# Two decoder layers on one core: the p product's groups issued between the seven products of the first gate/up blocks

## The chip, the cores and the metric

The kernel runs on one core of a Trainium2 chip. The metric is the device time of one execution in microseconds, the median of several runs; lower is better.

## What is computed

Two layers of a decoder trunk over 512 positions with width 1024, in float32. Each layer has a mixer (spatial gating, retention, forgetting attention), a gated MLP with a causal convolution of width 3 on the gate branch, and a last step that multiplies a projection of a per-layer input `p` with a gate:

```python
mix = jnp.concatenate([out_a.astype(dt), out_b, out_c], axis=-1) @ w_o[i]
x = x + rmsnorm(mix, mix_post_g[i])

h = rmsnorm(x, ffn_pre_g[i])
f = conv_gated_mlp(h, w_gate[i], w_up[i], conv_w[i], conv_b[i], w_down[i])
x = x + rmsnorm(f, ffn_post_g[i])

gate = jax.nn.sigmoid(rmsnorm(x, ple_pre_g[i]) @ w_ple_gate[i])
e = p[i] @ w_ple_proj[i]
x = x + rmsnorm(e * gate, ple_post_g[i])
```

The product that the change moves is `e = p[i] @ w_ple_proj[i]`: 512 x 256 times 256 x 1024. It depends on inputs alone and is needed only in the layer's last step.

## The kernel before

**Precision.** Each float32 operand is split into a high half (a cast on ScalarE, ACT) and a low half (a subtraction on VectorE, DVE) by `split` (line 648). Each product of two 128-deep operands is then three matmuls: high by high, high by low, low by high (`mm3`, line 908).

**The p product.** `embed_operands` (line 1352) loads and splits p and the weights. `embed` (line 1386) makes the product in groups, one for each half of 512 columns and each chunk of 128 positions: 6 matmuls of 512 columns into a PSUM bank named eps, a copy on ACT to a tile e, and a store of e to DRAM on SyncE's queue (SP). Layer 0 makes one column half there (4 groups, 24 matmuls; the other half has been made at the start of the program), layer 1 both (8 groups, 48 matmuls). `ffn` (line 1250) calls `embed` ahead of its loop over blocks.

**The MLP.** `ffn` has 32 gate/up blocks. Each makes 128 columns of gate and 128 of up for all 512 positions by seven block products in place of eight (`seven`, line 860), of 12 matmuls of 256 columns each, into three banks: beta, alpha, gamma. The order of the seven, by the operand of the activations, is b11 (beta), b21 (alpha), h6 (beta), hd (gamma), h7 (beta), b22 (gamma), h4 (beta). In the profile b11, b21 and b22 read hb, h6, h7 and h4 read hh, and hd reads hhd. Between products ACT and DVE copy the banks' partial sums out to gs and us, since a product that adds to the same bank has to wait for the copy. The weights of a block come as raw tiles (graw, two loads of 512 KB on SP), two adds by GpSimd's DMA (POOL), and splits into wg, wu, wsa and wsb. From block 4 on, matmuls of the down projection (bank dn, weights traw and thl) stand between the products; blocks 0 to 3 have none.

**The operands of the seven products** come from the normed activations in chunks of 128 positions, in the order 0, 2, 1, 3 (`Seven`, line 754). Each chunk is scaled on DVE (h), transposed on TensorE (PE, two groups of four into a bank hps), and split. Chunks 0 and 1 give b11 and b21; chunks 2 and 3, with 0 and 1, give h6, hd, h7, b22 and h4. So b11 and b21 are whole after chunk 1, and the other five after chunk 3.

**The order of the work.** Instructions are not issued as the code is written: they are recorded, and `Plan.issue` (line 252) orders each engine's by a model of durations. Among instructions that are ready and for which a buffer is free, the one recorded first goes first. PE is bound to the recorded order only from block 4 on (`plan.fence(True)`, line 1329). A tile is given out only to instructions within a distance of the oldest unfinished one, by the stage (`AHEAD`, line 62: 503 for emb, 443 for gu0). The order is fixed when the program is built; each engine then runs its own list, and waits where an operand is not there. Every recorded operation bears line 452 in the profile, so it is read by the names of tiles.

Of the kernel before, what the change touches and what calls it, by code (L numbers as in the profile page):

```python
# [39 lines left out]
NCH = 4  # L40
# [491 lines left out]
def body(ctx, tc, a, out):  # L532
    nc = tc.nc
    plan = Plan(tc)
# [18 lines left out]
    def bank(name="ps"):  # L553
        return ppt([P, 512], F32, tag="ps", name=name, bufs=8)
# [4 lines left out]
    def b8(name, shape, dt=F32):  # L559
        kind = "W" if name in ("wg", "wsa", "wsb") else "X" if dt == F32R else None  # L560
        return b8t([P] + list(shape), dt, name, kind)
# [295 lines left out]
        split(sb[:, 0, :], sb[:, 1, :], raw[:, 1024:2048])  # L857
        return wg, wu, sa, sb

    def seven(h, ws, gs, us, scale=1.0, between=None):  # L860

        wg, wu, sa, sb = ws
        be, al, ga = (bank(n)[:, 0:256] for n in ("beta", "alpha", "gamma"))
        t1, t2 = slice(0, 256), slice(256, 512)

        def product(ps, w, n, first, last, part=range(4)):
            for k in part:
                ks = slice(k * P, k * P + P)
                mm3(ps, lambda i: w[i][:, ks], lambda i: h.part(n, i, k), first and k == 0, last and k == 3, True)

        def part(t, i):
            return [t[:, j, i * 512:i * 512 + 512] for j in range(2)]
        product(be, part(wg, 0), "b11", True, False)
        A.copy(gs[:, t1], be)
        product(al, part(wg, 1), "b21", True, True)
        V.tensor_tensor(out=gs[:, t1], in0=al, in1=gs[:, t1], op=ALU.add)
        product(be, part(sa, 0), "h6", False, False)
        A.copy(gs[:, t2], be)
        product(ga, part(sa, 1), "hd", True, False)
        if scale == 1.0:  # L880
            A.copy(us[:, t2], ga)
        else:
            A.mul(us[:, t2], ga, -scale)
        product(be, part(sb, 0), "h7", False, False)
        V.scalar_tensor_tensor(out=us[:, t2], in0=be, scalar=-scale, in1=us[:, t2], op0=ALU.mult, op1=ALU.subtract if scale == 1.0 else ALU.add)
        product(ga, part(sb, 1), "b22", False, True)
        V.tensor_tensor(out=gs[:, t2], in0=ga, in1=gs[:, t2], op=ALU.add)
        rest = between() if between else None
        product(be, wu, "h4", False, True, range(1) if rest else range(4))
        if rest:  # L890
            rest()
            product(be, wu, "h4", False, True, range(1, 4))
        A.mul(us[:, t1], be, -scale)
# [14 lines left out]
    def mm3(ps, lhs, rhs, first, last, skip=False):  # L908
        for i, (h, r) in enumerate(((0, 0), (0, 1), (1, 0))):
            T.matmul(ps, lhsT=lhs(h), rhs=rhs(r), start=first and i == 0, stop=last and i == 2, skip_group_check=skip)  # L910
# [339 lines left out]
    def ffn(l, hs, emb, ready, x, new, g, nxt):  # L1250
# [7 lines left out]
        facc = []  # L1258
        acts = {}

        def gate_up(b, between):
            ws = gate_up_weights(l, b) if b not in ready else ready[b]
            gs, us = wk("gs"), wk("us")
            seven(hs, ws, gs, us, between=between)

            cv = wk("cv")
            A.activation(cv, gs, AF.Identity, bias=cw[:, 3, b:b + 1], scale=cw[:, 2, b:b + 1])
            V.scalar_tensor_tensor(out=cv[:, 1:S], in0=gs[:, 0:S - 1], scalar=cw[:, 1, b:b + 1], in1=cv[:, 1:S], op0=ALU.mult, op1=ALU.add)
            V.scalar_tensor_tensor(out=cv[:, 2:S], in0=gs[:, 0:S - 2], scalar=cw[:, 0, b:b + 1], in1=cv[:, 2:S], op0=ALU.mult, op1=ALU.add)
            A.activation(cv, cv, AF.Gelu_apprx_tanh)  # L1270
            V.tensor_tensor(out=cv, in0=cv, in1=us, op=ALU.mult)
            if b % 2 == 0:
                acts[b // 2] = b8("act", (2, 2, S), F32R)
            t = acts[b // 2]
            split(t[:, 0, b % 2, :], t[:, 1, b % 2, :], cv)
# [44 lines left out]
                rest = down(q - 1, c, units[q, hf], add)  # L1320
            return rest

        plan.stage = "emb"
        embed(l, *emb)
        plan.stage = "gu0"
        for b in range(31):
            if b == 4:
                plan.stage = "gu"
                plan.fence(True)
            gate_up(b, lambda: pieces(b))  # L1330
        plan.fence(False)
        gate_up(31, lambda: None)
        pieces(31)()
# [2 lines left out]
        us = [wd(7, hf) for hf in range(2)]  # L1336
# [46 lines left out]
                plan.fence(not c2)  # L1383
        return pT, us

    def embed(l, pT, us, chunks=range(NCH)):

        for hf, u in us.items():
            cs = slice(hf * 512, hf * 512 + 512)
            e = b8("e", (NCH, 512))  # L1390
            for c in chunks:
                ps = bank("eps")
                ts = slice(c * P, c * P + P)
                for k in range(2):
                    mm3(ps, lambda i: pT[:, i, k, ts], lambda i: u[:, i, k, :], k == 0, k == 1)
                A.copy(e[:, c, :], ps)
                SY.dma_start(out=ed[l][:, c, cs], in_=e[:, c, :])

    ov = out[0].rearrange("(c p) d -> p c d", p=P)

# [91 lines left out]
    for l in range(DEPTH):  # L1492
# [3 lines left out]
        hs = Seven(g)  # L1496
        emb = out_proj(l, cc, ready, Rows(src), xd[3 * l], g, hs)
# [36 lines left out]
```

## Time and profile before

| | us |
|---|---|
| timed runs, median of 3 | 1567.31 |
| lowest and highest timed run | 1564.96, 1567.66 |
| profiled execution, span from the first to the last instruction | 1564.8 |
| PE busy, DVE busy, ACT busy, POOL busy | 1546.8, 1219.5, 888.6, 193.3 |
| p product of layer 1 on PE, first to last start | 1012.8 to 1024.5 |

The page gives no time for the profiled execution other than its span. In rows of the profile, "beta<-hb,wg" means that bank beta is written from operand hb and weights wg; a bracket at the end says how long the engine had been idle before the row and what ended that. PEld is the loading of weights into TensorE, SPq and POOLq are queues of DMA issues. A start is given in us from the start of the span.

### The profile page before, as it was taken

The numbers are of one execution on the slowest core, as the hardware profiler recorded it, in microseconds if no ns is written. First come the engines' busy times: TensorE is split into PE (matmuls) and PEld (weight loads), VectorE is DVE, ScalarE is ACT, GpSimd is POOL, SyncE is SP. The second block draws the span as 40 slices with busy tenths as digits, with TensorE's granted clock in tenths as the row PEclk, the third lists the DMA queues.
The fourth block names the chain that finished last, engine by engine and source line by source line (L and its number), as shares of the span: only waits on it lengthen the run. The fifth ranks groups of instructions, "written<-read, shape, count | busy, mean of one in ns | idle before, by whom it ended". The sixth has DMA issues, their size and how long they took to land.

```text
span 1564.8 us, 26898 instructions
## 1 busy us (share of the span) xinstructions
PE 1546.8 (99%) x10554; PEld 1401.3 (90%) x10554; DVE 1219.5 (78%) x2036; ACT 888.6 (57%) x1501; POOL 193.3 (12%) x233
## 2 busy tenths in 40 slices
PE   9999999999999999999999999999999999999997
PEld 6998878999899999998889898799999999999986
DVE  6778978977778778767796789799677788687685
ACT  8556647765554545535584576586555455455362
POOL 1111112101101111000120101121101011011010
PEclk9999999999999999999999999999999999999999
DMA  9444529545637446456474346295546455455641
GB/s 331 92 123 104 180 90 291 134 121 142 169 81 198 137 96 176 130 156 247 155 216 102 85 122 210 76 301 136 145 112 155 143 136 147 128 150 148 232 158 54
DMA packets 87877, 239.00 MB, mean 153 GB/s; under 512 B 10036, under 2 KB 18364, under 8 KB 87752
## 3 DMA queue, kind: packets, MB, share of 16 engines
q1 hardware_dynamic: 64856, 195.81, 36.0%
q0 software_dynamic: 22464, 40.90, 16.4%
q8 instruction: 82, 1.34, 0.3%
q10 hardware_dynamic: 432, 0.59, 0.1%
q14 instruction: 43, 0.35, 0.1%
HBM read 219.94 MB, written 17.33 MB: 152 GB/s over the span
## 4 chain that ended last, share of the span: by engine, by line
PE 91%; ACT 3%; DMA 3%; DVE 2%; issue 1%; SPq 0%; POOLq 0%; POOL 0%; DVEq 0%; ACTq 0%
PE beta L452 26%; PE dn L452 21%; PE ps L452 14%; PE gamma L452 13%; PE alpha L452 6%; PE wo L452 3%; DMA graw<-in_w_gu_dram 2%; PE hps L452 1%; PE sps L452 1%; PE tps L452 1%; PE ops L452 1%; PE eps L452 1%; PE gps L452 1%; ACT thl L452 1%; PE rops L452 1%
## 5 line engine op out<-in xcount | busy, mean ns | idle before, releaser
L452 PE MATMUL dn<-thl,act 128*128 128x512 f32 x1536 | 370.5, 391 | 0.0
L452 PEld LDWEIGHTS dn<-thl,act 128*128 128x128 f32 x1536 | 280.4, 188 | 52.3
L452 PE MATMUL ps<-thl,hT 128*128 128x512 f32 (+3 forms) x984 | 209.7, 368 | 1.1 <-ACT hT L452 0.9
L452 POOL DMA_DIRECT2D graw<-in_w_gu_dram x128 | 112.4, 917 | 759.0 <-DVE wg L452 162.2
L452 PEld LDWEIGHTS ps<-thl,hT 128*128 128x128 f32 x984 | 175.1, 188 | 25.0 <-ACT hT L452 1.5
L452 DVE TENSOR_TENSOR thl<-traw,thl 128x1024 fp32r<-128x1024 f32 (+3 forms) x124 | 142.3, 1155 | 19.3 <-ACT thl L452 19.2
L452 ACT CAST thl<-traw 128x1024 fp32r<-128x1024 f32 (+3 forms) x124 | 121.3, 995 | 22.0 <-DVE wsb L452 8.9
L452 PEld LDWEIGHTS beta<-hh,wu 128*128 128x128 f32 x936 | 125.6, 188 | 9.1
L452 PE MATMUL beta<-hh,wu 128*128 128x256 f32 x936 | 130.2, 279 | 0.0
L452 PE MATMUL beta<-hh,wsa 128*128 128x256 f32 x936 | 122.0, 279 | 1.2 <-ACT gs L452 0.8
L452 PE MATMUL beta<-hh,wsb 128*128 128x256 f32 x936 | 120.5, 278 | 2.0 <-ACT gs L452 1.5
L452 PE MATMUL gamma<-hhd,wsa 128*128 128x256 f32 x936 | 121.7, 278 | 0.0
L452 DVE TENSOR_TENSOR wsb<-graw,wsb 128x1024 fp32r<-128x1024 f32 x78 | 95.3, 1222 | 29.5 <-PE beta L452 16.8
L452 PEld LDWEIGHTS beta<-hh,wsa 128*128 128x128 f32 x936 | 113.4, 188 | 2.6 <-ACT gs L452 1.4
L452 PEld LDWEIGHTS beta<-hh,wsb 128*128 128x128 f32 x936 | 112.9, 188 | 2.8 <-ACT gs L452 2.1
L452 DVE TENSOR_TENSOR graw<-graw 128x512 f32<-128x512 f32 x156 | 106.3, 686 | 10.8 <-DMA graw<-in_w_gu_dram 8.3
L452 PEld LDWEIGHTS gamma<-hhd,wsa 128*128 128x128 f32 x936 | 113.8, 188 | 0.0
L452 DVE TENSOR_TENSOR facc<-dn,facc 128x512 f32<-128x512 f32 x112 | 77.0, 687 | 45.1 <-PE dn L452 44.8
L452 DVE TENSOR_TENSOR wg<-graw,wg 128x1024 fp32r<-128x1024 f32 x78 | 95.2, 1220 | 15.8 <-ACT wg L452 8.7
L452 DVE TENSOR_TENSOR wsa<-graw,wsa 128x1024 fp32r<-128x1024 f32 x78 | 95.2, 1220 | 14.7 <-ACT wsa L452 14.6
L452 PE MATMUL beta<-hb,wg 128*128 128x256 f32 x768 | 100.5, 278 | 1.3 <-DVE hb L452 0.8
L452 DVE SCALAR_TENSOR_TENSOR cv<-gs,cw,cv 128x511 f32<-128x511 f32 (+1 forms) x128 | 95.3, 745 | 7.5 <-ACT cv L452 7.1
(225 smaller groups left out, 2625.4 us busy)
## 6 DMA issues: line engine op xcount, KB each, us to landing
graw<-in_w_gu_dram SPq DMA_DIRECT2D x128, 512.0 KB
graw<-in_w_gu_dram POOLq DMA_DIRECT2D x128, 256.0 KB, 5.4
traw<-in_w_dn_dram SPq DMA_DIRECT2D x64, 512.0 KB
x<-x SPq DMA_DIRECT2D x40, 512.0 KB
graw<-in_w_fm_dram SPq DMA_DIRECT2D x28, 512.0 KB
traw<-in_w_wo_dram SPq DMA_DIRECT2D x16, 512.0 KB
traw<-in_w_pg_dram SPq DMA_DIRECT2D x16, 512.0 KB
graw<-in_w_fm_dram POOLq DMA_DIRECT2D x28, 256.0 KB, 4.7
```

The lines of the kernel that those rows point to most:

```text
L452: made = o[1](*[self.map(v) for v in o[2]], **{k: self.map(v) for k, v in o[3].items()})
```

## The change

`embed` becomes a generator, `embed_pieces`, that stops after each group. `ffn` makes the generator and gives it to the first four blocks; `seven` draws one group from it behind its second product and one behind its fourth. So eight groups at most are recorded in blocks 0 to 3; layer 0 has four, which go to blocks 0 and 1. They are recorded under the stage gu0, no longer emb.

```diff
-    def seven(h, ws, gs, us, scale=1.0, between=None):
+    def seven(h, ws, gs, us, scale=1.0, between=None, wide=None):
...
         product(al, part(wg, 1), "b21", True, True)
         V.tensor_tensor(out=gs[:, t1], in0=al, in1=gs[:, t1], op=ALU.add)
+        if wide is not None:
+            next(wide, None)
         product(be, part(sa, 0), "h6", False, False)
         A.copy(gs[:, t2], be)
         product(ga, part(sa, 1), "hd", True, False)
...
             A.mul(us[:, t2], ga, -scale)
+        if wide is not None:
+            next(wide, None)
         product(be, part(sb, 0), "h7", False, False)
...
-        def gate_up(b, between):
+        def gate_up(b, between, wide=None):
             ws = gate_up_weights(l, b) if b not in ready else ready[b]
             gs, us = wk("gs"), wk("us")
-            seven(hs, ws, gs, us, between=between)
+            seven(hs, ws, gs, us, between=between, wide=wide)
...
-        plan.stage = "emb"
-        embed(l, *emb)
+        wide = embed_pieces(l, *emb)
         plan.stage = "gu0"
         for b in range(31):
             if b == 4:
                 plan.stage = "gu"
                 plan.fence(True)
-            gate_up(b, lambda: pieces(b))
+            gate_up(b, lambda: pieces(b), wide if b < 4 else None)
...
-    def embed(l, pT, us, chunks=range(NCH)):
+    def embed_pieces(l, pT, us, chunks=range(NCH)):
 
         for hf, u in us.items():
             cs = slice(hf * 512, hf * 512 + 512)
-            e = b8("e", (NCH, 512))
+            e = None
             for c in chunks:
+                e = b8("e", (NCH, 512)) if e is None else e
                 ps = bank("eps")
...
                 SY.dma_start(out=ed[l][:, c, cs], in_=e[:, c, :])
+                yield
+
+    def embed(*args):
+        for _ in embed_pieces(*args):
+            pass
```

What the planner makes of it: every engine's order is the same in both programs up to the gate/up blocks of layer 1. PE in layer 1, from chunk 1's second transposes, before (the number behind a name tells tiles apart; beta_11078 is block 0's bank, hps_11092 and hps_11105 are chunk 3's transposes):

```order
L452 MATMUL hps_11021<-k_ident_80,h_11006 128x128 x4
L452 MATMUL eps_11004<-ehl_10611,pT_10595 128x512 x2
L452 MATMUL eps_11032<-ehl_10611,pT_10595 128x512 x6
L452 MATMUL eps_11047<-ehl_10611,pT_10595 128x512 x6
L452 MATMUL eps_11058<-ehl_10611,pT_10595 128x512 x6
L452 MATMUL beta_11078<-hb11_10823,wg_10663 128x256 x8
L452 MATMUL hps_11092<-k_ident_80,h_11076 128x128 x4
L452 MATMUL beta_11078<-hb11_10823,wg_10663 128x256 x3
L452 MATMUL hps_11105<-k_ident_80,h_11088 128x128 x4
```

And in the changed program, from the same row (beta_11043 and alpha_11068 are block 0's, beta_11046 and alpha_11108 block 1's; hps_11119 and then hps_11130 are chunk 3's):

```order
L452 MATMUL hps_11021<-k_ident_80,h_11006 128x128 x4
L452 MATMUL eps_11004<-ehl_10611,pT_10595 128x512 x2
L452 MATMUL eps_11035<-ehl_10611,pT_10595 128x512 x3
L452 MATMUL beta_11043<-hb11_10823,wg_10663 128x256
L452 MATMUL beta_11046<-hb11_10823,wg_11018 128x256
L452 MATMUL eps_11035<-ehl_10611,pT_10595 128x512 x2
L452 MATMUL beta_11043<-hb11_10823,wg_10663 128x256 x11
L452 MATMUL alpha_11068<-hb21_10838,wg_10663 128x256
L452 MATMUL beta_11046<-hb11_10823,wg_11018 128x256 x3
L452 MATMUL alpha_11068<-hb21_10838,wg_10663 128x256 x11
L452 MATMUL beta_11046<-hb11_10823,wg_11018 128x256 x8
L452 MATMUL alpha_11108<-hb21_10838,wg_11018 128x256 x6
```

Thirteen matmuls of p have left this place, and 42 matmuls of blocks 0 and 1 stand ahead of chunk 3's first transposes, where 8 stood; behind chunk 3's second transposes (hps_11130) follow three alpha_11108, eleven of block 2's beta, and then the first with hhd. Of the matmuls that left, one stands behind block 0's h6 product, six ahead of block 3's h6 and six ahead of its h7. ACT in the same stretch, from the copy of the first eps of the second half, before:

```order
L452 COPY e_11060<-eps_11004 128x512
L452 COPY e_11060<-eps_11032 128x512
L452 COPY e_11060<-eps_11047 128x512
L452 CAST wg_11080<-graw_10947 128x1024
L452 COPY e_11060<-eps_11058 128x512
L452 CAST wu_11103<-graw_10947 128x512
L452 COPY s22_11115<-hps_11105 128x512
L452 COPY gs_11124<-beta_11078 128x256
L452 CAST hb22_10909<-s22_11115 128x4x128
L452 CAST hhd_10905<-sd_11118 128x4x128
L452 CAST hh7_10943<-s7_11129 128x4x128
L452 CAST hh6_10926<-s6_11139 128x4x128
```

And in the changed program (wg_11070 is block 2's gate weights, wg_11166 block 3's):

```order
L452 CAST wg_11070<-graw_10933 128x1024
L452 COPY gs_11084<-beta_11043 128x256
L452 CAST wu_11089<-graw_10933 128x512
L452 COPY e_11096<-eps_11004 128x512
L452 COPY gs_11111<-beta_11046 128x256
L452 COPY s22_11140<-hps_11130 128x512
L452 CAST hhd_10905<-sd_11128 128x4x128
L452 CAST hb22_10909<-s22_11140 128x4x128
L452 CAST wg_11166<-graw_11023 128x1024
L452 CAST hh6_10926<-s6_11154 128x4x128
L452 CAST hh7_10946<-s7_11180 128x4x128
```

Three copies of e have left, block 2's cast stands ahead, and block 3's cast has come ahead of h6's. On DVE, in the same way, block 2's wg now comes ahead of chunk 3's two h. SP in layer 1, from the stores of e's first column half, before:

```order
L452 DMA e_10964<-e 128x512 x4
L452 DMA x_10787<-x 128x1024
L452 DMA graw<-in_w_gu_dram 128x1024
L452 DMA e_10964<-e 128x512 x3
L452 DMA graw<-in_w_gu_dram 128x1024
L452 DMA e_10964<-e 128x512
L452 DMA graw<-in_w_gu_dram 128x1024 x2
L452 DMA traw<-in_w_dn_dram 128x1024 x2
L452 DMA graw<-in_w_gu_dram 128x1024 x4
L452 DMA traw<-in_w_dn_dram 128x1024 x2
```

And in the changed program:

```order
L452 DMA e_10964<-e 128x512 x4
L452 DMA graw<-in_w_gu_dram 128x1024 x2
L452 DMA x_10787<-x 128x1024
L452 DMA e_10964<-e 128x512
L452 DMA graw<-in_w_gu_dram 128x1024
L452 DMA e_10964<-e 128x512
L452 DMA graw<-in_w_gu_dram 128x1024
L452 DMA traw<-in_w_dn_dram 128x1024 x2
L452 DMA graw<-in_w_gu_dram 128x1024 x4
L452 DMA traw<-in_w_dn_dram 128x1024
L452 DMA e_10964<-e 128x512
L452 DMA traw<-in_w_dn_dram 128x1024
```

Block 3's two loads have come ahead of the store of x; the four stores of e's second half stand apart, one ahead of each of block 4's two loads, and one on each side of the last load of traw shown.

## The prediction

> **What bounds the kernel now.** I read the page's busy line first, then the busy time by stretches of the second layer, then PE's waits, then the rows of each engine around the p product.
>
> ```profile
> PE 1546.8 (99%) x10554; PEld 1401.3 (90%) x10554; DVE 1219.5 (78%) x2036; ACT 888.6 (57%) x1501; POOL 193.3 (12%) x233
> ```
>
> TensorE (PE) is busy for 1546.8 of 1564.8 us, so only the 18 us in which it is idle can be won without removing matmuls, and the change removes none. Where is that idle time? The stretches below show the window, then its length and PE's busy time, (instructions), the same for weight loads, DVE, ACT and POOL, and last the clock, DMA share and GB/s. The two run from the first product of p in layer 1 to block 7 of the gate/up blocks:
>
> ```profile
> 1012.80:1024.73 11.93, 11.93 (x58) 9.89 (x57) 10.49 (x18) 10.86 (x22) 4.59 (x6) 1.00 1.00 325
> 1024.73:1120.00 95.27, 95.26 (x746) 91.97 (x745) 82.32 (x117) 66.29 (x105) 14.36 (x17) 1.00 0.67 184
> ```
>
> PE has no idle time in the first and 0.01 us in the second. From 1075 us to the end PE waits for another engine once, 0.6 us for an ACT copy:
>
> ```profile
> PE beta L452 <- ACT gs L452: 0.6, 1, 0.6
> ```
>
> So in layer 1 PE is full where the p product stands, and full behind it.
>
> **What the change moves.** The order of the changed program is the same as before on every engine through layer 0: there the four groups of p (24 matmuls) stand in one piece ahead of the first block in both. In layer 1, 33 of 48 matmuls of p still come ahead of the first gate/up matmul; two come two matmuls later, one inside block 0, and twelve in block 3, six ahead of its third product and six ahead of its fifth. So the change, in effect, takes 15 matmuls, about a third of the second layer's p product, out of the piece that stands between chunk 1's and chunk 3's transposes, and moves products of blocks 0 and 1 forward into the hole. No instruction is added or removed on PE. The sum of its work is unchanged, and the question is only whether the products that move forward find their operands.
>
> *The gap behind chunk 1's transposes.* PE's rows of layer 1 (start, length, what):
>
> ```profile
> 1012.80 6.16 PE L452 MATMUL eps<-ehl,pT 128*128 128x512 f32 x26
> ...
> 1019.71 0.60 PE L452 MATMUL hps<-k_ident,h 128*128 128x128 f32 x4
> 1020.06 4.84 PE L452 MATMUL eps<-ehl,pT 128*128 128x512 f32 x20
> 1024.73 1.11 PE L452 MATMUL beta<-hb,wg 128*128 128x256 f32 x8
> 1025.85 0.66 PE L452 MATMUL hps<-k_ident,h 128*128 128x128 f32 x4
> ```
>
> Twenty p matmuls take 1024.73 - 1020.06 = 4.67 us, 0.2335 each, and today they cover the splitting of chunk 1. Thirteen of them go. What they cover, on ACT, DVE and POOL:
>
> ```profile
> 1020.00 0.58 ACT L452 CAST hb<-hps 128x512 fp32r<-128x512 f32 x1
> ...
> 1021.09 0.69 DVE L452 TENSOR_TENSOR hb<-hps,hb 128x512 fp32r<-128x512 f32 x1 [0.29 <-ACT bt L452]
> ...
> 1022.83 0.68 DVE L452 TENSOR_TENSOR hb<-hps,hb 128x512 fp32r<-128x512 f32 x1
> ...
> 1022.96 1.58 ACT L452 COPY e<-eps 128x512 f32<-128x512 f32 x3
> ...
> 1024.12 0.89 POOL L452 TENSOR_TENSOR rs<-vh,minus_half 128x1 f32<-128x1 f32 x1
> 1024.38 1.11 ACT L452 CAST wg<-graw 128x1024 fp32r<-128x1024 f32 x1
> ...
> 1025.04 1.42 DVE L452 SCALAR_TENSOR_TENSOR h<-x,rs,gain 128x512 f32<-128x512 f32 x2 [1.46 <-POOL rs L452]
> ```
>
> And layer 0, which already runs without the second half's matmuls, so that its products of blocks 0 and 1 follow chunk 1's transposes as they now will in layer 1:
>
> ```profile
> 251.88 0.38 PE L452 MATMUL beta<-hb,wg 128*128 128x256 f32 x1 [0.29 <-ACT hb L452]
> ...
> 252.35 0.69 DVE L452 TENSOR_TENSOR hb<-hps,hb 128x512 fp32r<-128x512 f32 x1 [0.54 <-ACT bt L452]
> ...
> 253.09 1.54 PE L452 MATMUL beta<-hb,wg 128*128 128x256 f32 x11 [0.83 <-DVE hb L452]
> ...
> 256.59 0.77 PEld L452 LDWEIGHTS beta<-hb,wg 128*128 128x128 f32 x6 [0.34 <-DVE wg L452]
> ...
> 258.19 0.60 PE L452 MATMUL hps<-k_ident,h 128*128 128x128 f32 x4
> ...
> 260.27 0.28 PE L452 MATMUL gamma<-hhd,wsa 128*128 128x256 f32 x1
> ...
> 262.25 0.68 DVE L452 TENSOR_TENSOR hh<-s,hh 128x512 fp32r<-128x512 f32 x1
> ...
> 263.57 1.46 PE L452 MATMUL beta<-hh,wsa 128*128 128x256 f32 x11
> ```
>
> ```profile
> 257.00:294.00 37.00, 37.00 (x317) 37.00 (x317) 36.32 (x57) 28.40 (x47) 7.96 (x9) 1.00 0.83 248
> ```
>
> The last row gives the pace of the 256-wide matmuls, 37.00 / 317 = 0.117 us. Walking the new order on PE from 1020.06 with these two paces:
> - Five p matmuls, 1.17 us, to 1021.23. The first beta needs the high half of hb, done at 1020.00 + 0.58 = 1020.58. No wait.
> - Two beta matmuls and two of p, 0.23 + 0.47, to 1021.93. The next beta needs the low half, done at 1021.09 + 0.69 = 1021.78; in layer 0 the same step was done at 252.35 + 0.69 = 253.04 and PE began at 253.09, a hand-over of 0.05. Spare 0.10.
> - Eleven beta, one alpha, three beta, 1.76, to 1023.69. The next alpha needs the low half of the other hb, 1022.83 + 0.68 = 1023.51. Spare 0.13 after the hand-over.
> - Twenty-five matmuls, 2.93, to 1026.62: chunk 3's first transposes, 0.77 later than at present. Their h now stands on DVE behind the low half of block 2's gate weights. That needs ACT's cast, which moves ahead of the copies of e, from 1024.38 to about 1022.96, done by 1024.07; DVE's half (1.23 us, taking the length of ACT's 1.11 and a little) ends by about 1025.3. POOL's rs is there at 1024.12 + 0.89 = 1025.01, so h runs from 1025.3, its first half ready near 1026.0. Spare 0.6.
> - From there layer 0 is the pattern. Second transposes to the first hhd matmul: 260.27 - 258.19 = 2.08 us there, and 0.35 + 14 x 0.117 = 1.99 here. To the low half of h6: 263.57 - 258.19 = 5.38 there, 0.35 + 39 x 0.117 = 4.91 here, with the operand done 262.25 + 0.68 - 258.19 = 4.74 after the transposes. Spare 0.1 after the hand-over. Layer 0 had no wait at all in the 37 us from 257 to 294.
>
> So the walk gives no wait, with spares of 0.1 us in three places. One or two will miss: I put 0.1 us on the sum. The two ends are 0 and what layer 0 lost with no p matmul as cover, 0.29 + 0.83 + 0.34 = 1.46 us; 0.1 is nearest to the first, since here seven p matmuls (1.64 us) and a beta stay as cover and the two 0.29 and 0.83 are about that long together.
>
> *The other half.* The twelve matmuls in block 3 stand where PE had no wait, so they cover nothing; if they are late they delay nothing either, since e is read only when the layer's next stage begins. Their copies on ACT, 0.5 us each, move from a stretch in which PE was full to another. Each store of e on SP now stands ahead of later weights: the second one ahead of block 4's second half, the last two ahead of w_down's and blocks 7 and 8's. Those loads were issued tens of us ahead of their use; I cost this at 0 and let the slower rival hold it.
>
> *What can be won.* Below nothing, the sum is bounded by PE's waits behind 1012.8 us: 0.01 + 0.6 = 0.6 us, if the reordered ACT also loses that one wait.
>
> Sum: 1564.8 + 0.1 = 1564.9 us of span. The median of the timed runs, 1567.31, lies 2.5 us above the profiled span; I take that as what lies around it. So 1567.4.
>
> **Rivals.**
>
> *Layer 0's waits come back* (spares of 0.1 us are gone in several places): +0.6 to +1.5, up to 1568.8 us. For it: the three spares. Against: the cover above.
>
> *Slower: block 3's weights.* On ACT the cast of block 3's gate weights now stands ahead of the casts of h6, h7 and h4, on which every later product hangs. If its load is late, ACT stops, and PE with it. In layer 0 the like cast starts 260.35 - 258.19 = 2.16 us behind the second transposes; here these start at 1026.62 + 0.35 + 0.35 (three alpha between) = 1027.32, so ACT asks at 1029.5 us. The cast, the load's two halves, POOL's adds and how fast the DMA moved (last number, GB/s):
>
> ```profile
> 260.35 1.05 ACT L452 CAST wg<-graw 128x1024 fp32r<-128x1024 f32 x1
> ```
>
> ```profile
> 1020.64 0.39 SPq L452 DMA_DIRECT2D graw<-in_w_gu_dram  x1
> ...
> 1025.28 0.49 SPq L452 DMA_DIRECT2D graw<-in_w_gu_dram  x1
> ```
>
> ```profile
> 1018.04 0.91 POOL L452 DMA_DIRECT2D graw<-in_w_gu_dram  x1
> 1020.24 0.88 POOL L452 DMA_DIRECT2D graw<-in_w_gu_dram  x1 [1.29 <-DMA graw<-in_w_gu_dram]
> 1023.55 0.87 POOL L452 DMA_DIRECT2D graw<-in_w_gu_dram  x1 [2.44 <-ACT e L452]
> ```
>
> ```profile
> 1010.00:1015.00 5.00, 5.00 (x24) 4.06 (x23) 5.00 (x8) 5.00 (x11) 0.00 (x0) 1.00 0.64 174
> 1015.00:1020.00 5.00, 5.00 (x27) 4.15 (x26) 5.00 (x10) 3.93 (x8) 2.54 (x3) 1.00 0.99 365
> 1020.00:1025.00 5.00, 5.00 (x26) 4.17 (x25) 3.29 (x6) 5.00 (x11) 2.32 (x3) 1.00 1.07 353
> 1025.00:1030.00 5.00, 4.99 (x44) 4.79 (x43) 4.96 (x8) 4.10 (x9) 1.13 (x3) 1.00 1.07 299
> ```
>
> Both halves are now issued ahead of the store of x, near 1020.3. Up to and with them SP has issued, from 1010.8 on, 512 KB of x, four halves of 512 KB, four stores of e of 256 KB and these two halves, 4.72 MB, and POOL three adds of 256 KB, 0.79 MB. The rows move 0.87 + 1.83 + 1.77 = 4.46 MB by 1025 and the other 1.05 MB in 3.5 us: all is moved by 1028.5, 1.0 us before ACT asks. What landing adds is in no row; over 1.0 us of it, ACT waits. At the worst the load is as late as its second half was before, 1025.28 - 1020.3 = 5 us: landed by 1033.5, a wait of 4 us, and 1571.4 us. The Trainium skill, "DMA: Bandwidth & Descriptors", section "Anatomy of one DMA — SWDGE (gpsimd) path", gives about 2.0 us of fixed cost for each DMA, most of it the receipt of the last write; by that (an estimate) ACT would wait 1.0 us and the sum would be 1568.4. No row quoted here shows it.
>
> *Clock.* PE could be throttled while it hops between open groups. The opening of the program shows what slow matmuls cost:
>
> ```profile
> 1.47 6.25 PE L452 MATMUL idle<-idle 128*128 128x512 bf16 x16 [1.47 <-POOL idle L452]
> ```
>
> Sixteen take 0.39 us each against 0.2335: 2.5 us for one such bout, 1569.9. Against it: layer 0 hops between more groups and its clock reads 1.00 throughout. The Trainium skill, "TensorE: Matmul & The Clock Gate", section "A second HAM failure mode: psum-queue depth-cycling", says that cycling through PSUM banks can make the clock gate oscillate; by that rule the trace does not agree here.
>
> *Faster by mechanism*: the 0.6 us wait goes, 1566.8 us.
>
> **Numbers.** No new wait worth 0.6 us: 0.67. Layer 0's waits: 0.17. Slower by late weights or stores: 0.08. Faster by 0.6: 0.07. Clock: 0.01. A measurement of this kernel tells 0.2%, 3.1 us, from no change. Only the late-weights case lies beyond it. The three timed runs spread over 2.7 us by themselves (1564.96 to 1567.66), so a median may lie 0.2% off either way: I move 0.05 to faster and 0.03 to slower. That gives faster 0.05, same 0.84, slower 0.11. The range runs from the faster case less half that spread, 1566.8 - 1.35 = 1565.4, to the layer-0 case and as much, 1570.2; it leaves out the late weights and the clock's far end.
>
> **What would show it.** Right: in the new trace PE shows no idle over 0.2 us at any row from 1020 to 1070; block 0's first beta begins near 1021.2 and chunk 3's transposes near 1026.6; ACT's cast of block 3's weights begins without a DMA wait near 1029.5; layer 0 reads as before. Wrong: a wait of PE on DVE hb like layer 0's 0.83, an ACT row that waits for DMA graw, a clock below 1.00, or a new wait of PE in blocks 4 to 8, behind SP's stores.

## The result and the profile after

| | before | after |
|---|---|---|
| median of the timed runs, us | 1567.15 (7 runs, 1564.96 to 1568.37) | 1571.86 (7 runs, 1569.36 to 1575.22) |
| span of the profiled execution, us | 1564.8 | 1567.7 |

The ratio is 1.0032 [1.0023, 1.0041]: slower by 0.3%, and above the range of the prediction. The profiled execution of the changed kernel took 1569.36 us, the fastest of its seven, so its trace shows 2.9 us (1567.7 - 1564.8) of the 4.7; the other 1.8 us need more executions, shown further down.

The page's busy line of the changed kernel: PE does the same work.

```profile
PE 1546.5 (99%) x10554; PEld 1400.7 (89%) x10554; DVE 1219.6 (78%) x2036; ACT 887.7 (57%) x1501; POOL 193.2 (12%) x233
```

The stretches of the changed kernel, with one more that the prediction did not read (columns as in the prediction: length, then PE's busy time):

```profile
1012.80:1024.73 11.93, 11.93 (x73) 10.43 (x72) 11.15 (x19) 10.80 (x22) 4.57 (x6) 1.00 1.02 340
1024.73:1120.00 95.27, 95.11 (x734) 91.01 (x733) 82.06 (x118) 66.02 (x106) 13.95 (x17) 1.00 0.65 177
1120.00:1320.00 200.00, 195.73 (x1405) 182.78 (x1404) 150.24 (x207) 104.60 (x161) 23.20 (x27) 1.00 0.55 146
```

The last of them before:

```profile
1120.00:1320.00 200.00, 199.39 (x1422) 185.88 (x1421) 154.40 (x212) 106.19 (x163) 23.59 (x27) 1.00 0.54 145
```

PE is as full as before where the p product was moved, and idle for 200.00 - 195.73 = 4.27 us between 1120 and 1320 us, against 0.61 before. No matmul was moved there. PE's waits in the changed kernel from the start of layer 1's gate/up stage on (us in total, times, longest):

```profile
PE beta L452 <- ACT gs L452: 4.3, 2, 2.6
...
PE beta L452 <- DVE us L452: 0.2, 1, 0.2
```

So there are three places: one copy to us, and two to gs. First the place that the prediction walked, on PE and for ACT's cast of block 3's weights:

```profile
1012.28 6.19 PE L452 MATMUL eps<-ehl,pT 128*128 128x512 f32 x26
...
1019.56 1.42 PE L452 MATMUL eps<-ehl,pT 128*128 128x512 f32 x5
1020.82 0.41 PE L452 MATMUL beta<-hb,wg 128*128 128x256 f32 x2
1021.06 0.62 PE L452 MATMUL eps<-ehl,pT 128*128 128x512 f32 x2
1021.52 1.41 PE L452 MATMUL beta<-hb,wg 128*128 128x256 f32 x11
...
1026.13 0.63 PE L452 MATMUL hps<-k_ident,h 128*128 128x128 f32 x4
```

```profile
1029.21 1.05 ACT L452 CAST wg<-graw 128x1024 fp32r<-128x1024 f32 x1
```

From the p matmuls behind chunk 1's transposes to chunk 3's transposes it is 1026.13 - 1019.56 = 6.57 us; the walk gave 1026.62 - 1020.06 = 6.56, and each of its steps holds to 0.1 us. No row of PE from 1012 us to the one at 1063 has a bracket, so nothing waits there, and ACT's cast has none either.

**Block 3, at 1063 us.** DVE before, then DVE, POOL and PE after:

```profile
1047.02 1.22 DVE L452 TENSOR_TENSOR wg<-graw,wg 128x1024 fp32r<-128x1024 f32 x1
...
1053.43 1.23 DVE L452 TENSOR_TENSOR wsa<-graw,wsa 128x1024 fp32r<-128x1024 f32 x1
```

```profile
1047.52 1.22 DVE L452 TENSOR_TENSOR wsa<-graw,wsa 128x1024 fp32r<-128x1024 f32 x1
...
1051.48 1.22 DVE L452 TENSOR_TENSOR wg<-graw,wg 128x1024 fp32r<-128x1024 f32 x1
...
1060.79 0.69 DVE L452 TENSOR_TENSOR graw<-graw 128x512 f32<-128x512 f32 x1 [0.50 <-DMA graw<-in_w_gu_dram]
...
1062.54 0.42 DVE L452 SCALAR_TENSOR_TENSOR us<-beta,us 128x256 f32<-128x256 f32 x1
```

```profile
1053.33 0.87 POOL L452 DMA_DIRECT2D graw<-in_w_gu_dram  x1 [5.08 <-ACT wu L452]
```

```profile
1063.01 1.69 PE L452 MATMUL beta<-hh,wu 128*128 128x256 f32 x12 [0.15 <-DVE us L452]
```

Read it from the bottom. PE's h4 product of block 3 waits for DVE's copy us. That copy stands in DVE's row behind an add on a raw weight tile (graw), and the add waits for GpSimd's transfer, issued at 1053.33 behind DVE's split of block 4's wg. Before, that split stood ahead of block 3's wsa (1047.02 against 1053.43); now it stands behind it. The bracket of GpSimd's row names ACT's cast wu; but in the kernel that is mended at this place, below, the transfer goes out 3.9 us ahead of that cast, and 0.63 us behind the end of the split as it does here, so it is the split that lets it go. In this execution the price is 0.15 us.

The two loads behind that place went out later as well, on SP, before and after:

```profile
1031.69 5.54 SPq L452 DMA_DIRECT2D graw<-in_w_gu_dram  x4
```

```profile
1040.28 12.28 SPq L452 DMA_DIRECT2D graw<-in_w_gu_dram  x4
```

In the old plan block 5's raw tile took the buffer of p and block 6's that of e; p and its split weights are now read until block 3, so both got other buffers, which came free later.

**Block 8, at 1129 us.** DVE and PE after:

```profile
1126.52 1.42 DVE L452 TENSOR_TENSOR graw<-graw 128x512 f32<-128x512 f32 x2 [4.69 <-DMA graw<-in_w_gu_dram]
1127.85 0.68 DVE L452 TENSOR_TENSOR cv<-cv,us 128x512 f32<-128x512 f32 x1
```

```profile
1129.51 1.68 PE L452 MATMUL beta<-hh,wsa 128*128 128x256 f32 x12 [1.69 <-ACT gs L452]
```

DVE waited 4.69 us for a load and then made cv, ACT made act from it and then the copy gs for which PE waits 1.69 us. Before, DVE made the same cv ahead of an add that waited for its load:

```profile
1126.45 0.69 DVE L452 TENSOR_TENSOR cv<-cv,us 128x512 f32<-128x512 f32 x1 [1.05 <-ACT us L452]
...
1132.89 0.69 DVE L452 TENSOR_TENSOR graw<-graw 128x512 f32<-128x512 f32 x1 [1.38 <-DMA graw<-in_w_gu_dram]
```

**Block 20, at 1312 us.** ACT and PE after, then ACT before:

```profile
1310.92 1.04 ACT L452 CAST thl<-traw 128x1024 fp32r<-128x1024 f32 x1 [2.99 <-DMA traw<-in_w_dn_dram]
1311.88 0.61 ACT L452 CAST act<-cv 128x512 fp32r<-128x512 f32 x1
1312.39 0.36 ACT L452 COPY gs<-beta 128x256 f32<-128x256 f32 x1
```

```profile
1312.81 1.65 PE L452 MATMUL beta<-hh,wsa 128*128 128x256 f32 x12 [2.58 <-ACT gs L452]
```

```profile
1308.60 0.62 ACT L452 CAST act<-cv 128x512 fp32r<-128x512 f32 x1 [0.25 <-DVE cv L452]
1309.13 0.37 ACT L452 COPY gs<-beta 128x256 f32<-128x256 f32 x1
...
1311.13 1.04 ACT L452 CAST thl<-traw 128x1024 fp32r<-128x1024 f32 x1
```

The cast of w_down's tile starts at 1311 in both, since its load lands then. Before, the copy gs stood ahead of it; now it stands behind, and PE waits for the cast with it.

The order of the blocks' starts agrees: the changed kernel is 0.90 us ahead at block 4 (0.52 of it from an earlier start of the stretch, 1012.28 against 1012.80), loses 2.14 at block 8 and 2.87 at block 20, wins 1.15 where before had its own wait, and ends 2.99 us behind.

### The profile page after: what moved, and what is told of

It reads as the page before. It is cut to its first block, busy times and chain, and to the rows that moved or that the text cites. A ratio compares the mean times of both kernels' runs of the same rounds, so it can differ in the third digit from the quotient of the medians.

```text
span 1567.7 us, 26901 instructions
## 1 busy us (share of the span) xinstructions
PE 1546.5 (99%) x10554; PEld 1400.7 (89%) x10554; DVE 1219.6 (78%) x2036; ACT 887.7 (57%) x1501; POOL 193.2 (12%) x233
## 4 chain that ended last, share of the span: by engine, by line
PE 89%; ACT 3%; DVE 3%; DMA 3%; issue 2%; POOL 0%; SPq 0%; POOLq 0%; DVEq 0%; ACTq 0%
PE beta L452 25%; PE dn L452 21%; PE ps L452 14%; PE gamma L452 12%; PE alpha L452 6%; PE wo L452 3%; DMA graw<-in_w_gu_dram 2%; PE hps L452 1%; DMA traw<-in_w_dn_dram 1%; PE eps L452 1%; PE sps L452 1%; PE tps L452 1%; PE ops L452 1%; PE gps L452 1%; ACT thl L452 1%
## 5 line engine op out<-in xcount | busy, mean ns | idle before, releaser
L452 ACT ACTIVATE cv<-cv 128x512 f32<-128x512 f32 x64 | 40.5, 633 | 111.7 <-DVE cv L452 111.7
```

The source lines that it names most:

```text
L452: made = o[1](*[self.map(v) for v in o[2]], **{k: self.map(v) for k, v in o[3].items()})
```

## The experiments

Three theories stood at the start. **Theory 1**: the planner redrew the orders of DVE and ACT for the rest of the layer, and in the new orders some steps that rest on a late load stand ahead of a step that PE wants. **Theory 2**: SP's moved stores of e hold the loads back. **Theory 3**: the p matmuls between the products are themselves to blame, by what they take from the blocks. A kernel that moves instructions of the finished order does so in a function `rearranged` that `Plan.issue` calls ahead of emission; `later(a, y)` puts a, and what rests on it, behind y. Below only its body is shown, under the kernel from which it departs. Before was run beside each group of experiments and had medians of 1567.09 to 1567.15 us (23 to 33 runs); beside the last three runs it ran once, in 1564.67 us.

### Undoing one part each

**The last 15 matmuls of p and their ACT copies put back ahead of block 0**, all other orders as after:

```diff
+    late = found[1][3:] + found[2] + found[3]      # eps matmuls of groups 6, 7, 8
+    order = [i for i in order if i not in late and i not in copies]
+    k = order.index(found[1][2]) + 1
+    order[k:k] = late
+    k = order.index(cast)                          # ACT: block 2's wg
+    order[k:k + 1] = [*copies[:3], cast, copies[3]]
```

> The changed kernel with the fifteen p matmuls of layer 1 that had moved (the rest of group 6, groups 7 and 8) put back ahead of the first block, and ScalarE's four copies of the second half of e with them; SP's order, and all that VectorE and ScalarE do from block 4 on, stay as the change has them. Theory 1 (the order that the planner gives VectorE and ScalarE behind block 4 costs the time, not the moved matmuls): the two late waits of TensorE on the gs copy stay, about 1.7 and 2.6 us at blocks 8 and 20, and the time stays at the changed kernel's 1571.9 or goes up by the 0.4 to 0.9 us that the changed kernel gained before block 4: 1571.5 to 1573. Theory 2 (SP's four late stores of e hold up the loads): they stay where they are, so also 1571.9. Theory 3 (the moved matmuls themselves cost the time in blocks 0 to 3): back to 1567.2, under 1569.

Measured: 1577.31 us (6 runs), 1.0060 [1.0043, 1.0076] of before, 5.5 us above the changed kernel and outside what any theory gave. In the profiled execution, the slowest of the six, the DVE add of block 3 waits 2.67 us for GpSimd's transfer, and PE 4.24 behind it, in rows of DVE and PE:

```profile
1067.46 0.69 DVE L452 TENSOR_TENSOR graw<-graw 128x512 f32<-128x512 f32 x1 [2.67 <-DMA graw<-in_w_gu_dram]
```

```profile
1069.67 2.72 PE L452 MATMUL beta<-hh,wu 128*128 128x256 f32 x11 [4.24 <-DVE us L452]
```

Theory 3 falls: the time goes up. The twelve p matmuls in block 3 had given the late transfer cover. Without them it goes out at 1058.09, 4.8 us later than in the changed kernel, while PE is ready for the product 2.6 us later (at 1065.43 against 1062.86). They were not without use, as the prediction had it. Three stretches at half the granted clock come on top in this execution; the last section returns to them.

**The last four stores of e issued from ACT's queue instead of SP's:**

```diff
+    for c in copies:
+        j = c + 1
+        ops[j] = ("ACT", self.tc.nc.scalar.dma_start, *ops[j][2:])
+        order.remove(j); order.insert(order.index(c) + 1, j)
```

> The changed kernel with the last four stores of e in layer 1 issued from ScalarE's queue, each behind its own copy, and no longer among SP's loads; all else in the changed kernel's order. Theory 1: the order of VectorE and ScalarE behind block 4 is the same, both gs waits stay within 0.5 us, 1571 to 1572.5. Theory 2: the loads of blocks 4 to 8 and of w_down go out earlier by SP's waits for the copies, the wait at block 8 goes, 1567 to 1570. Theory 3: 1571.9.

Measured: 1575.34 us (5 runs), 1.0054 [1.0042, 1.0066]. With no store between them, SP had traw out at 1028.30 and block 5's loads still at 1041.50 (after: 1040.28): they wait for a buffer, not for stores. One store had held back the second half of block 4's weights (out at 1035.04 in the changed kernel, by 1028.1 here), but the three waits stay: 1.77, 1.86 and 2.33 us. Theory 2 falls. The time also missed the 1571 to 1572.5 of theory 1; why it is 3.5 us above the changed kernel was not taken apart.

**The orders at blocks 8 and 20 mended**: at block 8 DVE's two graw adds go behind cv's last step and act's low half, and ACT's second thl cast behind the copy gs; at block 20 the first thl cast goes behind gs. The numbers are places in the recorded list:

```diff
+    order = later([10515, 10516], 10362)
+    order = later([10741], 10389)
+    order = later([12431], 12081)
```

> The changed kernel with nothing moved but, at block 8, VectorE's two adds of graw behind the act product and ScalarE's second cast of thl behind the gs copy, and at block 20 ScalarE's first cast of thl behind the gs copy. Theory 1: both waits of TensorE (1.69 and 2.58 us in the profiled execution) go, so 1571.9 - 4.3 = 1567.6; up to 1569 if something else is late behind them, down to 1566 if nothing is. Theory 2: the loads are still as late, and what needs the cast weights waits instead (the down projection, the next block's wsa): over 1570. Theory 3: no change, 1571.9.

Measured: 1569.41 us (11 runs), 1.0014 [1.0005, 1.0023], 2.45 us below the changed kernel. The three moves win half of the loss. It missed my 1567.6, as the wait at block 3 had grown to 2.23 us in this execution and 1.25 were left at 1316:

```profile
PE beta L452 <- DVE us L452: 2.2, 1, 2.2
PE beta L452 <- ACT gs L452: 1.9, 3, 1.2
```

**Before, with another order of DVE and ACT** (a planner's distance moved; PE and SP keep their order, DVE and ACT do not):

```diff
-    "gu": 478,
+    "gu": 470,
```

> The kernel before, p in one piece, with one number of the planner changed (how far ahead of the work the gate/up weights may be taken, 478 to 470): TensorE's, SP's and GpSimd's orders stay those of before, VectorE's and ScalarE's are drawn up anew in both layers. Theory 1: such a redraw alone moves the time by over 0.1%, through waits of TensorE on the gs copy that stand at other blocks than before: 1562 to 1573, not 1567.2 +- 1. Theories 2 and 3: nothing that they name has changed, 1567.2 +- 1.

Measured: 1567.48 us (11 runs), 1.0001 [0.9993, 1.0010]. My expectation missed. A redraw does not have to cost: this one has two PE waits in layer 1, 1.08 and 0.29 us. What costs is what the particular order puts ahead of what.

### Block 3

**As the mended kernel, and DVE's split of block 4's wg ahead of block 3's wsa and wsb, as it was before:**

```diff
+    order.remove(9802)
+    order.insert(order.index(9682), 9802)
```

> As the first mend, and also VectorE's split of block 4's wg (the low part) moved ahead of block 3's wsa and wsb, where the kernel before has it; nothing else differs from the changed kernel. Theory 1 (VectorE's and ScalarE's order, now in three places: at block 3 TensorE waits for us, which stands on VectorE behind an add that waits for GpSimd's second summing transfer of block 4, and that transfer may only start when this split has read its data): the transfer goes out some 4 us earlier, the wait of 0.15 us in the changed kernel's profile and 2.23 us in the first mend's goes, the spread of the times shrinks, and the time is 1569.4 - 2.2 = 1567.2 or, with the 0.4 to 0.9 us gained before block 4, down to 1566. Theory 4 (p's operands hold three large buffers until block 3, and the loads that must wait for them are late): the order doesn't help late loads, 1569 or more.

Measured: 1568.51 us (11 runs), 1.0011 [1.0002, 1.0020]. GpSimd's transfer went out at 1050.35, 3.0 us earlier than in the changed kernel. The wait at block 3, 2.23 us in the profile of the kernel mended at two places, is gone, and one of 0.34 us stands at 1053, in the block before. Rows of POOL and PE:

```profile
1050.35 0.88 POOL L452 DMA_DIRECT2D graw<-in_w_gu_dram  x1 [1.14 <-ACT us L452]
```

```profile
1053.04 1.65 PE L452 MATMUL beta<-hh,wu 128*128 128x256 f32 x12 [0.34 <-DVE us L452]
```

Of the 4.7 us, 3.35 are undone by four moves on DVE and ACT. The last 0.90 of them, between the two mended kernels, is not clear of noise (their intervals overlap); the profiles show the wait itself gone. I expected 1566 to 1567.2, so 1.4 us are not accounted for.

**The held buffers taken away** by letting the last two groups of p read another resident tile (a quarter of layer 1's e then holds another product, and goes through a small tile):

```diff
+    other = hs.t["h4"].rearrange("p i k n -> p i (k n)")    # for the last two groups
-    mm3(ps, lambda i: pT[:, i, k, ts], lambda i: u[:, i, k, :], k == 0, k == 1)
+    mm3(ps, lambda i: other[:, i, k * P:k * P + P], lambda i: other[:, i, k * 512:k * 512 + 512], k == 0, k == 1)
+    to = wk("ew")
```

> The changed kernel in which the last two groups of the p product of layer 1 multiply a tile that is resident anyway (instead of p and its weights) and put their result into a small tile: the same matmuls, copies and stores at the same places, with a different result in a quarter of e, and the buffers of p, of its second weights and of e free from block 0 on instead of block 3 on. VectorE's order up to block 4 comes out as in the changed kernel, so block 4's wg is still split behind block 3's sums. Theory 4 (held buffers): loads of blocks 5 and 6 go out up to 8 us earlier, and the time falls to 1567 to 1568.5. Theory 1 (order): the wait on us at block 3 stays, and the one at block 8 within 1 us: 1570.5 to 1573.

Measured: 1570.71 us (11 runs), 1.0022 [1.0013, 1.0031]. The loads of blocks 5 and 6 went out at 1038.47 and were all issued by 1041.9 (after: 1052.6), and the wait at block 3 is gone, though DVE's order is still the late one there:

```profile
1038.47 3.40 SPq L452 DMA_DIRECT2D graw<-in_w_gu_dram  x4
```

```profile
1063.14 1.58 PE L452 MATMUL beta<-hh,wu 128*128 128x256 f32 x12
```

GpSimd's transfer was issued at 1054.10, and the add behind it began at 1060.66 without a wait; in the kernel mended at two places it was issued at 1054.12, and the add could begin only at 1063.35. So, as far as one profile of each shows, block 3's wait needs both: the late split and the late loads, which move while GpSimd's transfer does. Blocks 8 and 20 keep their waits (1.95 and 2.20 us).

### How many blocks the groups are spread over

**Two groups in each of blocks 0 to 2, the last two behind block 2**, and **two groups in block 0, the other six right behind it**:

```diff
-            gate_up(b, lambda: pieces(b), wide if b < 4 else None)
+            gate_up(b, lambda: pieces(b), wide if b < N else None)
+            if b == N - 1:
+                for _ in wide:
+                    pass
```

N = 3:

> Two groups of p in each of the first three blocks and the last two behind block 2 (the changed kernel has them in block 3). p's buffers are held till block 2, almost as long, but VectorE's order around block 4 comes out as before the change: block 4's wg is split ahead of block 3's sums. Theory 1: no wait on us at block 3, so at most what the later blocks add: 1566.5 to 1569.5. Theory 4: buffers held nearly as long, so near the changed kernel, 1570 to 1572.

Measured: 1568.05 us (11 runs), 1.0004 [0.9995, 1.0013]. p's buffers are held until block 2, and there is no wait at block 3, which speaks for DVE's order there; the profile, of the fastest execution, has three waits on gs behind it (1.09 us the longest).

N = 1:

> Two groups of p within block 0 and the other six right behind it. p's buffers are free again in block 0, VectorE's order around block 4 as before the change. Theories 1 and 4 agree: no wait on us at block 3; 1566 to 1568.5. If the interleaving itself cost time (theory 3, against which the first run spoke), 1569 or more.

Measured: 1565.36 us (11 runs), 0.9985 [0.9977, 0.9994]: faster than before, if by less than the 0.2% that the prediction counts, and the best of all kernels here (I had expected 1566 to 1568.5). Its only wait from 1012 us on:

```profile
PE beta L452 <- ACT gs L452: 0.8, 1, 0.8
```

That is 0.2 us more than before's, so the gain is none of waits in this layer. The profile points to the pace, below, but no run shows that the pace alone makes the gain.

### One cast, and the pace

**Before, with a single instruction moved**: ACT's first thl cast of block 20 ahead of the cast act and the copy gs.

```diff
+    order.remove(thl)
+    order.insert(order.index(act), thl)
```

> The kernel before, p in one piece, with one instruction moved: on ScalarE, at block 20 of layer 1, the first cast of thl stands ahead of the act cast and the gs copy, where the changed kernel has it, and not two places behind them. Theory 1 (the order costs the time): the weights for that cast go out at 1304.7 in the profile of before and can't be there ahead of 1311, the gs copy would then end near 1312.8 or later where TensorE wants it near 1309.8: a wait of 2.5 to 5 us there, and 1567.1 + 2.5 to 5 = 1569.6 to 1572. If the order were harmless and the changed kernel's load the late part: under 1568.

Measured: 1571.80 us (11 runs), 1.0026 [1.0016, 1.0035], as expected: one cast moved past two instructions costs as much as the whole change. ACT, then PE, then the window of PE's product:

```profile
1310.85 1.04 ACT L452 CAST thl<-traw 128x1024 fp32r<-128x1024 f32 x1 [2.55 <-DMA traw<-in_w_dn_dram]
1311.80 0.61 ACT L452 CAST act<-cv 128x512 fp32r<-128x512 f32 x1
1312.32 0.36 ACT L452 COPY gs<-beta 128x256 f32<-128x256 f32 x1
```

```profile
1312.73 2.93 PE L452 MATMUL beta<-hh,wsa 128*128 128x256 f32 x12 [2.65 <-ACT gs L452]
```

```profile
1312.73:1315.46 2.73, 2.73 (x13) 2.73 (x13) 2.54 (x4) 0.90 (x1) 0.33 (x1) 0.50 0.76 215
```

It costs twice in this execution, the slowest of the eleven: 2.65 us of waiting, and a granted clock of 0.50 over the product behind it. Three other waits in it (0.60, 0.67 and 0.53 us; before's profile has one of 0.61) are not put down to the cast: two of them come ahead of it.

**Before, with the last group of p (6 matmuls) behind chunk 3's second transposes**, to try the pace that the one-block kernel has:

```diff
+    k = order.index(hps) + 1        # chunk 3's second transposes
+    order[k:k] = late               # the last group's six matmuls
```

> The kernel before with the last group of p (six 512-wide matmuls) behind chunk 3's second transposes instead of ahead of them, its copy of e behind the first gs copy; no order of VectorE, SP or GpSimd changes. Pace theory (the 256-wide products run at 0.118 us each from about 1027 to 1073 in the kernel before and at 0.113 in the kernel with the pieces in block 0, whose seven last p matmuls stand right behind those transposes): the products of blocks 0 to 4 take 0.113, 31 runs of 12 save 0.053 us each, 1567.1 - 1.6 = 1565.5. If the pace hangs on something else: 1567.1 +- 0.5, with 0.118 still.

Measured: 1568.14 us (11 runs; one of 1711 us among them does not move the median), 1.0002 [0.9993, 1.0011]. PE's rows in this kernel:

```profile
1025.65 0.66 PE L452 MATMUL hps<-k_ident,h 128*128 128x128 f32 x4 [1.36 <-DVE h L452]
...
1035.17 1.52 PE L452 MATMUL beta<-hh,wsb 128*128 128x256 f32 x12
1036.54 1.52 PE L452 MATMUL gamma<-hb,wsb 128*128 128x256 f32 x12
```

The pace changed, as was wanted: a product of 12 matmuls in 1036.54 - 1035.17 = 1.37 us. Chunk 3's transposes lost six matmuls of cover and waited 1.36 us for their h, about what the pace won up to 1060 us. My 1565.5 missed, as I read it for that wait.

**A general rule tried**, on the one-block kernel and on before: on DVE all graw adds and thl remainders that stand right ahead of cv's last step go behind it, on ACT all thl casts right ahead of act go behind gs, in both layers. In outline:

```diff
+    for x in cv_times_us:           # DVE
+        order = later(adds_and_remainders_just_ahead(x), x)
+    for y in act_casts:             # ACT
+        order = later(thl_casts_just_ahead(y), next_gs(y))
```

> The kernel with two groups of p in block 0 and six right behind it (1565.4), and in both layers: what VectorE has of graw adds and thl remainders directly ahead of the product of cv and us goes behind it, and ScalarE's casts of thl directly ahead of an act cast go behind the gs copy that follows. Theory 1: the remaining waits of TensorE on a gs copy (0.77 us at block 12 of layer 1, 0.86 in layer 0) go, down to 1563.7; if the moved work is late for what needs it, 1565 to 1566.

> The kernel before with the same exchange on VectorE and ScalarE as the run just named, p in one piece. Theory 1: its waits on a gs copy (0.61 us in layer 1, up to 0.9 in layer 0) go: 1565.6 to 1567.1. With that it says how much of the run just named comes from the exchange and how much from where p stands.

Measured: 1566.99 us (11 runs), 0.9995 [0.9986, 1.0004], and 1567.24 us (11 runs), 0.9997 [0.9988, 1.0006]. The first is 1.6 us worse than the kernel from which it departs: it has new waits of 0.35 us at 1054.5 and 1062.4. The second has no wait of PE left behind 1012 us, and the same time as before. Both are above what I expected. The rule is not worth having; what mends one place spoils another.

### The changed kernel once more

The first profile showed 2.9 us of the 4.7. **The changed kernel, unaltered, three times**, one profile each:

> The changed kernel once more, unaltered, for another profile: its profiled execution was the fastest of seven (1569.36 against a median of 1571.9). Theory 1 with half clock: the late waits are the same three (at block 3 between 0.1 and 2.3 us, at block 8 about 1.7 to 2, at block 20 about 2.2 to 2.6), and the 2.5 us between that execution and the median are a longer wait at block 3 or some 1.4 to 1.7 us at half the granted clock behind a wait of about 2 us or more: in a profile of an execution at 1571 to 1573 one of these must show. If neither shows, something else makes the difference.

> The same kernel and the same question as the run just named, with the same numbers expected: a second profile.

> The same kernel and the same question as the two runs just named, with the same numbers expected: a third profile.

| execution, us | block 3's wait | block 8's | block 20's | lowest clock of a 4-us window, 1012 to 1500 us |
|---|---|---|---|---|
| 1569.36 (the first) | 0.15 | 1.69 | 2.58 | 1.00 |
| 1572.75 | 0.80 | 1.86 | 1.99 | 0.57 |
| 1571.77 | 1.57 | 2.28 | 1.22 | 0.57 |
| 1579.51 | 2.91 | 1.65 | 3.32 | 0.57 |

The three places are the same in all four (two executions have another wait, of 0.24 and 0.35 us, near 1256 and 1260 us). The waits differ, and more than I had expected: block 8's goes to 2.28 us, block 20's from 1.22 to 3.32. The first profile happened to have the shortest wait at block 3 and no drop of the clock. In the last, PE's row at block 3, and the window around it:

```profile
1068.26 2.93 PE L452 MATMUL beta<-hh,wu 128*128 128x256 f32 x12 [2.91 <-DVE us L452]
```

```profile
1068.00:1072.00 4.00, 3.75 (x19) 3.75 (x20) 4.00 (x7) 3.20 (x5) 0.86 (x1) 0.57 0.92 236
```

A clock of 0.57 over 4 us is 3.4 us at half, 1.7 us lost where PE is full. The execution of 1571.77 us has 0.9 us more of waits than the first and one such stretch, and a span longer by 2.4 us; that of 1572.75 has 0.2 us more of waits and two stretches, and 3.4 us. So the rest of the loss is a longer wait at block 3 and half a clock behind some of the waits. The last execution had also lost 2.6 us before layer 1's p product began (at 1014.89 us), which this does not explain.

## Why the prediction was wrong

**Right: the gap behind chunk 1's transposes.** The walk held to 0.01 us over 6.6 us, and none of its three 0.1-us spares was missed: 0, where I took 0.1. The rival "layer 0's waits come back" did not happen. Nor did "block 3's weights": ACT's cast began at 1029.21 with no wait. The signs of being right that I had named for layer 1 hold in the first profile, which has no idle time over 0.2 us on PE from 1020 to 1070 us; but they looked only at the place of the edit, and the loss lies behind it. Even there it was luck of the execution: the other three wait 0.80 to 2.91 us at block 3.

**Wrong, the step that failed: "The other half".** The sum has one term, the 0.1 us of the gap, and all that comes behind the walk stands in it at 0. I wrote that the twelve matmuls in block 3 "cover nothing", and of the loads that moved, "I cost this at 0". Put back, with three more, they leave a wait of 4.24 us behind them. And the reading stopped at ACT's and DVE's orders around chunk 3. The orders change to the end of the layer, and three places in them cost 0.15 to 2.91, 1.65 to 2.28 and 1.22 to 3.32 us: a raw-weight add or a w_down cast, waiting for its load, ahead of the copy that PE's next product needs. By medians, mending two of them gives back 2.45 us of the 4.7; mending the third gives 0.90 more, which is within the noise.

**Wrong: the reason in the last sentence.** "A new wait of PE in blocks 4 to 8, behind SP's stores" came true in its place at block 8, and just ahead at block 3, but the waits stayed when the stores were taken off SP. The buffers that p still held had a part, at block 3; at blocks 8 and 20 it is the order, and block 20 lies far outside what I named.

**Wrong: what PE's busy time allows.** PE at 95.26 of 95.27 us told me where nothing could be won. It says nothing of how near the next wait is: before's block 20 was one ACT instruction from a loss of 4.65 us (1571.80 - 1567.15). The change kept the sum of PE's work, as I said, but I took only the moved products' operands as in question, and not the copies behind every later product.

**Clock.** I gave it 0.01, by hopping between open banks. The clock read 1.00 through the hopping of blocks 0 to 2 in every profile. It reads 1.00 over the program's opening too (1.47 to 7.72 us of before), so the slow matmuls there, from which I took the price of 2.5 us, are not a case of it. It did fall, to 0.57 over 4 us, behind new waits of PE, in three of four profiles of the changed kernel. A wait was priced at its own length; it can cost up to 1.7 us more.

**Open.** What the last 1.4 us between the mended kernel and before are: its profile shows 1.45 us of PE waits from 1012 us on against 0.61, and the gain of 0.38 us ahead of block 4 is gone, but no run takes this apart. Why the planner's list comes out in this order at blocks 8 and 20 was not tried either; only that the order is the cause was shown, by moving it.

## What to carry to other kernels

When a planner fixes the order, a change in one place is a new order for all that follows. Compare every engine's list to the end of the stage, and look for a step that rests on a transfer and stands ahead of a copy that the bound engine needs; price it at the load's lateness. A full engine shows that no wait is there now, not that there is room for one. A tile that is read longer holds its buffer longer, and the loads that would have taken it show the price many blocks on.

## What the hardware showed that was not expected

**Half the clock after short waits.** Behind PE waits of 1.86 us and more the granted clock often fell to a half, for 3.4 us (0.57 over 4 us, above) and once, behind the longest wait, for 6.8. Twelve 256-wide matmuls then took 2.73 us in place of 1.36 (window above, 0.50), 1.4 us lost. The profiles have fifteen waits of 1.86 to 4.24 us from 1012 us on, and the clock fell behind twelve of them. It did not behind 1.95, 2.23 and 2.58 us (the last in the first profile of the changed kernel), nor behind any shorter wait there, of which 1.65, 1.69 and 1.77 us are the longest. The Trainium skill, "TensorE: Matmul & The Clock Gate", section "HAM oscillation — how this bites in real kernels", gives the rule "no PE-idle gaps >~3.4µs". Here the trace does not agree: gaps of little over half that were enough. The same page's Part 1 says of the warm-up that the window runs freely and that the number of slow matmuls is run-variable, which goes with what the four executions show.

**Two paces at one clock.** 256-wide matmuls run either 12 in 1.36 us or 12 in 1.42, at a granted clock of 1.00 both times. Two neighbours on PE, before and in the one-block kernel:

```profile
1034.20 1.58 PE L452 MATMUL beta<-hh,wsb 128*128 128x256 f32 x12
1035.62 1.58 PE L452 MATMUL gamma<-hb,wsb 128*128 128x256 f32 x12
```

```profile
1033.69 1.52 PE L452 MATMUL beta<-hh,wsb 128*128 128x256 f32 x12
1035.05 1.52 PE L452 MATMUL gamma<-hb,wsb 128*128 128x256 f32 x12
```

The fast pace began behind six or seven 512-wide matmuls of p between chunk 3's transposes and the blocks, in two kernels, and it lasted until 1060 to 1073 us: some 25 products of 12 by 0.05 us are 1.3 us, the better part of the one-block kernel's gain of 1.8. But the order does not fix the pace: block 2's h7 product took 1050.14 - 1048.73 = 1.41 us in the first profile of the changed kernel, and 1050.60 - 1049.24 = 1.36 in the second. Nor do 512-wide matmuls always bring the fast one: behind six of them in block 3 the products ran slow in all four, and in three of these they had run fast just before. What decides it is open.
